# Differential heads weighed two at a time, with their scores in one run, out of one pool of six PSUM banks

## The chip, the cores and the metric

The kernel runs on one core of one Trainium2 chip. The metric is the device time of one execution in microseconds. The kernel before takes 2825.22 us, the median of three runs (2824.94 to 2826.13).

Engines are named as in the profile: PE is TensorE, PEld its weight loads, DVE is VectorE, ACT is ScalarE, POOL is GpSimd, SP is SyncE, which issues most DMAs here.

## The reference

A two-layer encoder for one sequence of 256 tokens with 2048 features, all in float32. Each layer runs two kinds of attention side by side on the same normed input, gates both, adds them to the stream, and then runs a SwiGLU feed-forward and a small gated embedding. What matters here is the first half of a layer:

```python
z = h @ w_in[i]          # [diff q | diff k | diff v | q-latent | kv-latent | rope key | gate_diff | gate_mla]
# A: differential attention, 8 heads, two softmax maps of 64 dimensions each
scores  = jnp.einsum('bqhcd,bkhcd->bhcqk', qb, kh) * 64 ** -0.5
probs   = jax.nn.softmax(scores, axis=-1)
weights = probs[:, :, 0] - lam * probs[:, :, 1]
od      = jnp.einsum('bhqk,bkhe->bqhe', weights, v)
od      = rmsnorm(od, g_subln[i], SUBLN_EPS) * (1.0 - lam_init)
# B: latent attention, 8 heads; q_nope, q_rope from the q-latent, k_nope, v from the kv-latent
scores  = (q_nope @ k_nope.T + q_rope @ k_rope.T) * 192 ** -0.5
merged  = sigmoid(ga) * (A @ w_branch_diff) + sigmoid(gb) * (B @ w_branch_mla)
x       = x + merged @ w_out[i]
```

## The kernel before

The stream is kept transposed: 16 tiles of 128 features by 256 tokens. Every large product has the weights as the stationary operand and the tokens as the moving one. To keep float32 accuracy with products of float32r, each number is split into a high and a low part. A tile of tokens holds both parts side by side (512 columns). For each block of 128 x 128 weights PE issues two matmuls: the weights' high part (`whi`) against all 512 columns (L226) and the weights' low part (`wlo`) against the 256 columns of the high part (L230). `product` does this over the 16 blocks of a column of weights, 32 matmuls into one PSUM bank; `joined` adds the two halves of that bank with an ACT copy and a DVE add.

Weights come in pieces of up to 1024 columns: SP issues the DMA, ACT writes `whi` (L201), DVE writes `wlo = w - whi` (the subtraction in `tt`, L78). There are four buffers for the raw piece and three for each part. PE can't start a piece before both parts are there, and ACT can't make the next `whi` before PE has let a buffer go.

The order on each engine is not the order of the program. A planner, run when the program is built (`schedule_with_timeline_sim=True`), goes through a simulated time with its own costs and at each step issues, for each engine, the earliest instruction of the program that is ready by then, if its buffer is free. Two helpers tie it: `keep_in_program_order` puts an instruction behind the one traced just before it on the same engine, and `issue_after` puts a block behind a given instruction.

In the attention stage of a layer these steps occur:

- `queries_keys(h)`: two products (queries and keys of a differential head), each followed by the partial rotary turn on DVE and the split into high and low part.
- `keys_up(n)`: two heads' keys of the latent attention, two short products of two blocks each.
- `queries_up(n)`: two heads' queries of the latent attention, two products of four blocks each.
- `gate`: a product and a scaling. Seven of them stand in this stage or right behind it, the others beside the latent heads.
- the shared rotary key: `narrow` (L414), then `rotated`.
- `settle(h0)`: the norm of four finished differential heads, with eight transposes (L716).

A differential head goes through `diff_weights` and `diff_out`. `diff_weights` computes two maps of scores, one from partitions 0 to 63 and one from 64 to 127 of the same tiles. Each map takes six matmuls with 64 rows (three products of high and low parts for each half of the queries), and the two maps alternate, so a head has a run of 12 (L428). Each map fills a bank of its own. Then DVE takes the row maxima (L434), ACT the exponentials with their sums (L437), DVE the reciprocals (L438), and the two maps are combined into `E[0]` (ACT L691, DVE in `stt`, L81). `diff_out` transposes the weights on PE (L446), copies them (ACT L451), multiplies with the values (PE L701) and takes the squares for the norm.

`pipelined` sets the order: the scores of head h + 1 are traced before the transposes of head h. The generator `beside` is asked for one step before the scores and one between the transposes and the outputs of each head, so that products stand in both places. The first scores come right after the queries and keys of head 1, before any step of `beside`.

PSUM has eight banks: four in the pool `ps_mm` for products and values, two in `ps_s` for scores, two in `ps_at` for transposes and outputs. The very end of the kernel takes two of the `ps_s` banks again for the transposes of the result.

Of the kernel before, what the change touches and what calls it, by code (L numbers as in the profile page):

```python
# [16 lines left out]
ALU = mybir.AluOpType  # L17
# [39 lines left out]
def encoder(ctx, tc, x, p, positions, cols, lams, wq, wk, wv, wcq, wckv, wkr, wga, wgb,  # L57
# [6 lines left out]
    wts = pool("wts")  # L64
    tmp = pool("tmp")
    stat = pool("stat")
    ps_mm = pool("ps_mm", 4, space=PSUM)
    ps_s = pool("ps_s", 2, space=PSUM)
    ps_at = pool("ps_at", 2, space=PSUM)

    def scratch(tag, bufs, n=T):
# [2 lines left out]
    def bank(ps=ps_at, tag="at", name="at", shape=(P, 2 * T)):  # L74
        return ps.tile(list(shape), F32, tag=tag, name=name)
# [178 lines left out]
    def joined(acc, o=None):  # L254
        t = scratch("join", 3)
        A.activation(t, acc[:, T:], AF.Copy)  # L256
        o = scratch("a", 4) if o is None else o
        tt(o, acc[:, :T], t, ALU.add)
        return o
# [117 lines left out]
    def rotated(a, c_, s_, o=None):  # L377
        if o is None:
            r = bank()[:, :T]
            PE.matmul(r, halves, a, start=True, stop=True)  # L380
        else:
            r = a
        t = scratch("sh", 2)
        V.stream_shuffle(t, r, SWAP16)
        tt(t, t, s_, ALU.mult)
        tt(a, r, c_, ALU.mult)
        tt(a, a, t, ALU.add)
        if o is None:
            hi, rest = krs
            A.activation(hi[:, :T], a, AF.Copy)  # L390
            for j in range(2):
                s, t = slice(64 * j, 64 * j + 64), slice(j * T, (j + 1) * T)
                tt(rest[s, t], a[s], hi[s, :T].bitcast(F32), ALU.subtract)
        else:
            A.activation(o.rearrange("p (h t) -> p h t", h=2), a.rearrange("p (h t) -> p h t", h=1).to_broadcast([P, 2, T]), AF.Copy)
            for j in range(2):
                s, t = slice(64 * j, 64 * j + 64), slice(j * T, (j + 1) * T)
                tt(o[64 - 64 * j : 128 - 64 * j, t], a[s], o[s, t].bitcast(F32), ALU.subtract)

    def narrow(src, us):  # L400


        acc = bank(ps_mm, "mm", "mm")
        w = wts.tile([P, PT * P], F32, tag="w32", name="w32", bufs=W_BUFS)
        nc.sync.dma_start(w, src)
        w = w.rearrange("p (c m) -> p c m", m=64)
        for a in range(0, NC, PT):
            both = wts.tile([P, PT * P + 64], F32R, tag="whi", name="whi", bufs=3)[:, : PT * P]
            hi, lo = (both.rearrange("p (c f m) -> p c f m", f=2, m=64)[:, :, f, :] for f in range(2))
            part = w[:, a : a + PT, :]  # L410
            A.activation(hi, part, AF.Copy)
            tt(lo, part, hi.bitcast(F32), ALU.subtract)
            for j in range(PT):
                PE.matmul(acc, both[:, j * P : (j + 1) * P], us[a + j], start=a + j == 0, stop=a + j == NC - 1)  # L414
        return acc
# [1 line left out]
    def three(q, k):  # L417
        return [(q[:, :T], k[:, T:]), (q[:, T:], k[:, :T]), (q[:, :T], k[:, :T])]

    def scores(*maps):  # L420


        Ss = [bank(ps_s, "S", "S", (P, 2, T)) for _ in maps]
        for b in range(2):
            for j in range(len(maps[0])):
                for S, pairs in reversed(list(zip(Ss, maps))):
                    q, k = pairs[j]
                    PE.matmul(S[:, b, :], q[:, b * P : (b + 1) * P], k, start=j == 0, stop=j == len(pairs) - 1)  # L428
        return Ss

    def exps(S, E, scale):
# [95 lines left out]
    for L in range(DEPTH):  # L527
# [45 lines left out]
        def queries_keys(h, *inside):  # L573
            for which, w in enumerate((wq, wk)):
                a = joined(product(w[L, h], ua, inside=(8, inside[which]) if inside else None))
                sh = scratch("sh", 2)
                V.stream_shuffle(sh, a, ROPE16)
                tt(sh, sh, sr, ALU.mult)
                tt(a, a, cr, ALU.mult)
                tt(a, a, sh, ALU.add)  # L580
                split(qk[h][which], a)
# [18 lines left out]
        def keys_up(n):  # L600
            for acc in pair(w_kn[L, n : n + 2], ckv):
                kn.append(operand(fb(len(kn), F32R)))
                split(kn[-1], joined(acc))
# [19 lines left out]
        queries_keys(0, lambda: lcols.append(norm([skv], KVR)), lambda: lcols.append(norm([sq], QR)))  # L623
        queries_keys(1, lambda: latent_norm(ckv, "g_kv_latent", rkv, lcols[0]), lambda: latent_norm(cq, "g_q_latent", rq, lcols[1]))

        def beside():

            for h in range(2, DH):
                if h < 6:
                    keys_up(2 * h - 4)  # L630
                elif h == 7:
                    rotated(joined(narrow(wkr[L], ua)), crm, srm)
                yield
                queries_keys(h)
                yield
            for n in (8, 0, 2, 10):
                if n == 0:
                    settle(0)
                gate(wga, gate_a, next(todo))
                queries_up(n)  # L640
                yield
            settle(4)
            for n in (4, 6):
                gate(wga, gate_a, next(todo))
                queries_up(n)
            gate(wga, gate_a, next(todo))

        def gate(w, store, n):
            tt(store(n), joined(product(w[L, n], ua)), R, ALU.mult)
# [27 lines left out]
            tc.add_manual_dep(si.ins, last_exp[0].ins.name, NO_SYNC, reason="one change of tables")  # L677


        fill = beside()  # L680
        od, ods = [], ub[:8]
        ssd = stat.tile([P, 2 * DH], F32, tag="ssd", name="ssd", bufs=1)

        def diff_weights(h):
            q, k = qk[h]
            E = [weights(), weights("E1")]
            halves = [slice(c * 64, (c + 1) * 64) for c in range(2)]
            r = [exps(S, e, 0.125) for S, e in zip(scores(*(three(q[d], k[d]) for d in halves)), E)]
            ts(r[1], r[1], neg_lam[:, L : L + 1], None, ALU.mult)
            for b in range(2):  # L690
                A.activation(E[0][:, b, :], E[0][:, b, :], AF.Copy, scale=r[0][:, b : b + 1])  # L691
                stt(E[0][:, b, :], E[1][:, b, :], r[1][:, b : b + 1], E[0][:, b, :], ALU.mult, ALU.add)
            return E[0]

        def diff_out(h, W):
            wt = turned(W)
# [30 lines left out]
                next(out, None)  # L727
                W = nxt

        pipelined(diff_weights, diff_out, DH, lambda: next(fill, None))  # L730
        for _ in fill:
            pass
        vm, = (v for v in values(w_v[L], ckv) if v is not None)


# [1 line left out]
        def mla_weights(h):  # L737
            E = weights()
            t = slice(h % 2 * T, (h % 2 + 1) * T)
            S, = scores(three(qn[h], kn[h]) + [(qr[h // 2][:, t], krs[1][:, t]), (qr[h // 2][:, t], krs[0][:, :T])])  # L740
            r = exps(S, E, MLA_SCALE)
            for b in range(2):
                ts(E[:, b, :], E[:, b, :], r[:, b : b + 1], None, ALU.mult)
            return E
# [176 lines left out]
    def store(b, q, o):  # L921
        tc.keep_in_program_order(nc.sync.dma_start(out[b, :, q * 2 * T : (q + 2) * 2 * T], o))

    def S_bank():
        return operand(bank(ps_s, "S", "S", (P, 2, T)))

    def mm_bank():
        return bank(ps_mm, "mm", "mm")

    def steps(which, n):  # L930
        for _ in range(n):
            tc.keep_in_program_order(next(which))
# [6 lines left out]
    column = factors(0)  # L939
    for which, n in ((column, 2), (third, 1), (second, 2), (third, 2), (column, 2)):  # L940
        steps(which, n)
    t0 = [transposed(0, q, get()) for q, get in enumerate((S_bank, S_bank, mm_bank, mm_bank))]
    t1 = [transposed(1, 0, mm_bank())]
    column = factors(1)
    t1.append(transposed(1, 1, mm_bank()))
# [6 lines left out]
    for j in range(2):  # L952
        tc.keep_in_program_order(scaled(parts_[j][:, right], t0[2 * j + 1], cols_[0], V))
        steps(column, 2)
        store(0, 2 * j, parts_[j])
    t1.append(transposed(1, 3, S_bank()))
    for j in range(2):
        tc.keep_in_program_order(scaled(parts_[2 + j][:, left], t1[2 * j], cols_[1], V))
        scaled(parts_[2 + j][:, right], t1[2 * j + 1], cols_[1], A)
# [89 lines left out]
```

## Time and profile before

| | |
|---|---|
| Time, median of three runs | 2825.22 us (2824.94 to 2826.13) |
| Profiled execution: its own time | 2825.27 us |
| Profiled execution: span, first to last instruction | 2823.5 us |
| Granted clock of TensorE | 0.999 |
| Busy: PE / PEld / DVE / ACT | 2815.7 / 2489.4 / 2080.0 / 1532.0 us |
| Matmuls with 64 rows (scores of the differential heads) | 192, in 16 runs of 12 |
| Differential stage, first layer | about 106 to 207 us from the span's start |
| The same, second layer | about 1510 to 1611 us |

Rows of the order of time give start, duration, engine, line and operation, the tiles written and read, shapes, and a count where neighbours are merged. The end of a matmul is modelled, and matmuls overlap, so the time that one holds PE is read from its start to the start of the next. Tile names are those of the program: `ua` and `ub` are the two sets of token tiles, `mm` and `S` PSUM banks, `at` a bank of `ps_at`. Rows of waits give who waited, for whom, the sum in us, the count and the longest. Rows that group instructions give the count, then the busy time and the mean in ns, then the idle time ahead of them.

### The profile page before, as it was taken

To read this page: it belongs to the slowest core of one execution; us is meant where nothing else is said; L and a number is where in the kernel's file an instruction comes from. 1 tells how busy PE (TensorE), PEld (TensorE's weight loads), DVE (VectorE), ACT (ScalarE), POOL (GpSimd) and SP (SyncE) were. 2 spreads that over 40 slices of the span, in tenths; PEclk is the share of its full clock that TensorE was granted. 3 is DMA by queue.
4 is the path that set the end of the run, shared out by engine and by line. 5 is a ranking of instruction groups with operands and counts; after the bars stand their busy time and mean duration, and the time that the engine had idled before them with its cause. 6 is when DMAs were issued, how large, how long until landed. Compare 5 with 4: busy or idle time off the path is not lost.

```text
span 2823.5 us, 43989 instructions
## 1 busy us (share of the span) xinstructions
PE 2815.7 (100%) x16691; PEld 2489.4 (88%) x16691; DVE 2080.0 (74%) x3566; ACT 1532.0 (54%) x2554; POOL 3.1 (0%) x17
## 2 busy tenths in 40 slices
PE   9999999999999999999999999999999999999999
PEld 8888988888888888888888889888888888888888
DVE  8898668776666666677869976687766666666777
ACT  7676546554444444455646765465544444444556
POOL 0000000000000000000000000000000000000000
PEclk9999999999999999999999999999999999999999
DMA  7545455555665566566554454555556655655654
GB/s 247 174 162 172 157 187 198 194 193 194 186 200 193 188 195 197 193 193 193 194 193 166 157 172 158 194 198 193 194 193 189 199 193 185 202 194 194 193 193 157
DMA packets 158180, 531.36 MB, mean 188 GB/s; under 512 B 17168, under 2 KB 25360, under 8 KB 157968
## 3 DMA queue, kind: packets, MB, share of 16 engines
q1 hardware_dynamic: 157536, 527.96, 56.8%
q8 instruction: 131, 2.15, 0.3%
q10 hardware_dynamic: 432, 0.59, 0.1%
q14 instruction: 81, 0.66, 0.1%
HBM read 526.39 MB, written 2.10 MB: 187 GB/s over the span
## 4 chain that ended last, share of the span: by engine, by line
PE 100%; DMA 0%; DVE 0%; ACT 0%; DVEq 0%; issue 0%
PE mm L226 61%; PE mm L230 31%; PE S L428 1%; PE mmv L501 1%; PE mmv L502 1%; PE mmv L503 1%; PE at L446 1%; PE at L701 1%; PE mm L848 0%; PE at L757 0%; PE mm L414 0%; PE at L716 0%; PE mmv L472 0%; DMA gcol<-in_cols 0%; PE at L339 0%; PE at L307 0%
## 5 line engine op out<-in xcount | busy, mean ns | idle before, releaser
L201 ACT ACTIVATE whi<-w 128x1024 fp32r<-128x1024 f32 (+2 forms) x1038 | 1064.3, 1026 | 1225.6 <-issue 592.8
L78 DVE TENSOR_TENSOR wlo<-w,whi 128x1024 fp32r<-128x1024 f32 (+2 forms) x1038 | 1225.7, 1181 | 645.7 <-ACT whi L201 635.1
L226 PE MATMUL mm<-ub,whi 128*128 128x512 f32 x3936 | 1340.5, 389 | 0.0
L226 PE MATMUL mm<-ua,whi 128*128 128x512 f32 x3712 | 1274.8, 390 | 0.0
L230 PE MATMUL mm<-ub,wlo 128*128 128x256 f32 x3936 | 1084.6, 276 | 0.0
L230 PE MATMUL mm<-ua,wlo 128*128 128x256 f32 x3712 | 1027.8, 277 | 0.0
L226 PEld LDWEIGHTS mm<-ub,whi 128*128 128x128 f32 x3936 | 737.7, 188 | 152.4
L226 PEld LDWEIGHTS mm<-ua,whi 128*128 128x128 f32 x3712 | 696.2, 188 | 141.2
L230 PEld LDWEIGHTS mm<-ub,wlo 128*128 128x128 f32 x3936 | 738.8, 188 | 1.3
L230 PEld LDWEIGHTS mm<-ua,wlo 128*128 128x128 f32 x3712 | 697.0, 188 | 1.9
L78 DVE TENSOR_TENSOR a<-mm,join 128x256 f32<-128x256 f32 (+1 forms) x423 | 174.9, 417 | 1.7 <-ACT join L877 1.4
L256 ACT ACTIVATE join<-mm 128x256 f32<-128x256 f32 x452 | 165.8, 368 | 6.5 <-PE mm L230 5.8
L78 DVE TENSOR_TENSOR xT<-xT,mm 128x256 f32<-128x256 f32 x256 | 106.9, 420 | 41.5 <-PE mm L230 37.6
L78 DVE TENSOR_TENSOR a<-a,row 128x256 f32<-128x256 f32 (+1 forms) x209 | 87.6, 422 | 5.9
L78 DVE TENSOR_TENSOR a<-a 128x256 f32<-128x256 f32 x120 | 50.9, 426 | 4.0
L78 DVE TENSOR_TENSOR ua<-a,ua 128x256 fp32r<-128x256 f32 x120 | 50.0, 418 | 1.0 <-ACT ua L264 1.0
L264 ACT ACTIVATE ua<-a 128x256 fp32r<-128x256 f32 x120 | 48.2, 403 | 2.6 <-DVE a L78 2.6
L437 ACT ACTIVATE E<-S,nm 128x256 f32<-128x256 f32 x96 | 44.2, 472 | 8.1 <-DVE nm L84 8.0
L501 PE MATMUL mmv<-whi,ua 128*128 128x512 f32 x124 | 47.2, 392 | 0.0
L502 PE MATMUL mmv<-whi,ua 128*128 128x512 f32 x124 | 47.0, 392 | 0.0
L503 PE MATMUL mmv<-wlo,ua 128*128 128x512 f32 x124 | 41.2, 391 | 0.0
L78 DVE TENSOR_TENSOR ssq<-ssq,sq 128x256 f32<-128x256 f32 x96 | 40.2, 419 | 0.3 <-ACT sq L294 0.3
(214 smaller groups left out, 1211.6 us busy)
## 6 DMA issues: line engine op xcount, KB each, us to landing
w<-in_w_gate SPq DMA_DIRECT2D x176, 512.0 KB, 4.5
w<-in_w_up SPq DMA_DIRECT2D x176, 512.0 KB, 4.6
w<-in_w_down SPq DMA_DIRECT2D x128, 512.0 KB, 4.2
w<-in_wga SPq DMA_DIRECT2D x64, 512.0 KB, 3.7
w<-in_wgb SPq DMA_DIRECT2D x64, 512.0 KB, 3.7
w<-in_w_out SPq DMA_DIRECT2D x64, 512.0 KB, 3.9
w<-in_w_pg SPq DMA_DIRECT2D x64, 512.0 KB, 4.7
w<-in_w_down SPq DMA_DIRECT2D x64, 384.0 KB, 3.6
```

The source lines that it names most:

```text
L78: return V.tensor_tensor(out=o, in0=a, in1=b, op=op)
L201: last_split[:] = A.activation(hi[:, s], w[:, s], AF.Copy), tt(lo[:, s], w[:, s], hi[:, s].bitcast(F32), ALU.subtract)
L226: lead = PE.matmul(acc, hi[:, s], u, start=start, stop=False)
L230: rest = PE.matmul(acc[:, T:], lo[:, s], u[:, :T], start=False, stop=stop)
L256: A.activation(t, acc[:, T:], AF.Copy)
L264: return A.activation(hi, src, AF.Copy), tt(lo, src, hi.bitcast(F32), ALU.subtract)
L428: PE.matmul(S[:, b, :], q[:, b * P : (b + 1) * P], k, start=j == 0, stop=j == len(pairs) - 1)
L437: last_exp[0] = A.activation(E[:, b, :], S[:, b, :], AF.Exp, bias=nm[:, b : b + 1], scale=scale, accum_out=sm[:, b : b + 1])
L446: PE.transpose(tp[:, kb, b * P : (b + 1) * P], W[:, b, kb * P : (kb + 1) * P], ident)
L501: PE.matmul(banks[k][b], xh, hi[:, s], start=c == 0, stop=False)
L502: PE.matmul(banks[k][b], xl, hi[:, s], start=False, stop=False)
L503: last_mm[:] = [PE.matmul(banks[k][b], xh, lo[:, s], start=False, stop=c == n - 1)]
```

## The change

The two pools `ps_mm` and `ps_s` become one of six banks, and scores take their banks from it. `diff_weights` takes two heads at once: `scores` allots four banks and issues the 12 matmuls of head h0 + 1 and then the 12 of head h0, each tied to the one before with `keep_in_program_order`. The softmax of both follows, then both heads' transposes and, later, both heads' outputs.

`beside` and the use of `pipelined` for these heads are replaced by a list written out. Queries and keys of head 2, the first `keys_up` and queries and keys of head 3 come before the first scores. Each pair has products between its scores and its transposes and again between its transposes and its outputs. The shared key stands beside the third pair, behind two gates, and `settle(0)` comes behind the scores of the last pair. The latent heads keep `pipelined`; their scores come from the pool of six, and are not tied. At the end of the kernel the transposes take banks of this pool.

```diff
-    ps_mm = pool("ps_mm", 4, space=PSUM)
-    ps_s = pool("ps_s", 2, space=PSUM)
+    ps_mm = pool("ps_mm", 6, space=PSUM)
...
-    def scores(*maps):
...
-        Ss = [bank(ps_s, "S", "S", (P, 2, T)) for _ in maps]
-        for b in range(2):
-            for j in range(len(maps[0])):
-                for S, pairs in reversed(list(zip(Ss, maps))):
-                    q, k = pairs[j]
-                    PE.matmul(S[:, b, :], q[:, b * P : (b + 1) * P], k, start=j == 0, stop=j == len(pairs) - 1)
+    def mm_bank():
+        return bank(ps_mm, "mm", "mm")
+
+    def S_bank():
+        return mm_bank().rearrange("p (b t) -> p b t", b=2)
...
+    def scores(*heads):
...
+        Ss = [[S_bank() for _ in maps] for maps in heads]
+        for banks, maps in zip(Ss, heads):
+            for b in range(2):
+                for j in range(len(maps[0])):
+                    for S, pairs in reversed(list(zip(banks, maps))):
+                        q, k = pairs[j]
+                        m = PE.matmul(S[:, b, :], q[:, b * P : (b + 1) * P], k, start=j == 0, stop=j == len(pairs) - 1)
+                        if len(heads) > 1:
+                            tc.keep_in_program_order(m)
         return Ss
...
-        def beside():
-
-            for h in range(2, DH):
-                if h < 6:
-                    keys_up(2 * h - 4)
-                elif h == 7:
-                    rotated(joined(narrow(wkr[L], ua)), crm, srm)
-                yield
-                queries_keys(h)
-                yield
-            for n in (8, 0, 2, 10):
-                if n == 0:
-                    settle(0)
-                gate(wga, gate_a, next(todo))
+        def shared_key():
+            rotated(joined(narrow(wkr[L], ua)), crm, srm)
+
+        def gate_and_queries(n=None):
+            gate(wga, gate_a, next(todo))
+            if n is not None:
                 queries_up(n)
-                yield
-            settle(4)
-            for n in (4, 6):
-                gate(wga, gate_a, next(todo))
-                queries_up(n)
-            gate(wga, gate_a, next(todo))
...
-        def diff_weights(h):
-            q, k = qk[h]
-            E = [weights(), weights("E1")]
+        def diff_weights(h0):
             halves = [slice(c * 64, (c + 1) * 64) for c in range(2)]
-            r = [exps(S, e, 0.125) for S, e in zip(scores(*(three(q[d], k[d]) for d in halves)), E)]
...
+            pairs = [[three(qk[h][0][d], qk[h][1][d]) for d in halves] for h in (h0 + 1, h0)]
+            Ws = []
+            for Ss in scores(*pairs):
+                E = [weights(), weights("E1")]
+                r = [exps(S, e, 0.125) for S, e in zip(Ss, E)]
...
+                Ws.append(E[0])
+            return Ws[::-1]
...
-        pipelined(diff_weights, diff_out, DH, lambda: next(fill, None))
-        for _ in fill:
-            pass
+        def work(*steps_):
+            for act, *arg in steps_:
+                act(*arg)
+
+        def weighed_pair(h, beside, ahead):
+            Ws = diff_weights(h)
+            work(*beside)
+            outs = [diff_out(h + j, Ws[j]) for j in range(2)]
+            for part in outs:
+                next(part)
+            work(*ahead)
+            for part in outs:
+                next(part, None)
+
+        Q, K, G = queries_keys, keys_up, gate_and_queries
+        work((Q, 2), (K, 0), (Q, 3))
+        weighed_pair(0, ((Q, 4), (K, 2)), ((Q, 5),))
+        weighed_pair(2, ((Q, 6), (K, 4)), ((Q, 7),))
+        weighed_pair(4, ((G, 8), (G,)), ((shared_key,), (K, 6)))
+        weighed_pair(6, ((settle, 0), (G, 0), (G, 2)), ((G, 10),))
+        settle(4)
+        work((G, 4), (G, 6))
...
-            S, = scores(three(qn[h], kn[h]) + [(qr[h // 2][:, t], krs[1][:, t]), (qr[h // 2][:, t], krs[0][:, :T])])
+            (S,), = scores([three(qn[h], kn[h]) + [(qr[h // 2][:, t], krs[1][:, t]), (qr[h // 2][:, t], krs[0][:, :T])]])
...
-    t0 = [transposed(0, q, get()) for q, get in enumerate((S_bank, S_bank, mm_bank, mm_bank))]
+    t0 = [transposed(0, q, get()) for q, get in enumerate((mm_bank, mm_bank, mm_bank, mm_bank))]
...
-    t1.append(transposed(1, 3, S_bank()))
+    t1.append(transposed(1, 3, mm_bank()))
```

More of the change, by code (lines that the diff above doesn't have):

```diff
@@ L418, in three @@
         return [(q[:, :T], k[:, T:]), (q[:, T:], k[:, :T]), (q[:, :T], k[:, :T])]
-    def scores(*maps):
-        Ss = [bank(ps_s, "S", "S", (P, 2, T)) for _ in maps]
-        for b in range(2):
-            for j in range(len(maps[0])):
-                for S, pairs in reversed(list(zip(Ss, maps))):
-                    q, k = pairs[j]
-                    PE.matmul(S[:, b, :], q[:, b * P : (b + 1) * P], k, start=j == 0, stop=j == len(pairs) - 1)
+    def mm_bank():
+        return bank(ps_mm, "mm", "mm")
+    def S_bank():
+        return mm_bank().rearrange("p (b t) -> p b t", b=2)
+    def three(q, k):
+        return [(q[:, :T], k[:, T:]), (q[:, T:], k[:, :T]), (q[:, :T], k[:, :T])]
+    def scores(*heads):
[8 more added lines that the diff above has]
+                            tc.keep_in_program_order(m)
         return Ss
@@ L677, in sigmoid @@
             tc.add_manual_dep(si.ins, last_exp[0].ins.name, NO_SYNC, reason="one change of tables")
-        fill = beside()
         od, ods = [], ub[:8]
         ssd = stat.tile([P, 2 * DH], F32, tag="ssd", name="ssd", bufs=1)
-        def diff_weights(h):
-            q, k = qk[h]
-            E = [weights(), weights("E1")]
+        def diff_weights(h0):
             halves = [slice(c * 64, (c + 1) * 64) for c in range(2)]
-            r = [exps(S, e, 0.125) for S, e in zip(scores(*(three(q[d], k[d]) for d in halves)), E)]
[L689 to L693, printed above, removed]
+            pairs = [[three(qk[h][0][d], qk[h][1][d]) for d in halves] for h in (h0 + 1, h0)]
[3 more added lines that the diff above has]
+                r = [exps(S, e, 0.125) for S, e in zip(Ss, E)]
+                ts(r[1], r[1], neg_lam[:, L : L + 1], None, ALU.mult)
+                for b in range(2):
+                    A.activation(E[0][:, b, :], E[0][:, b, :], AF.Copy, scale=r[0][:, b : b + 1])
+                    stt(E[0][:, b, :], E[1][:, b, :], r[1][:, b : b + 1], E[0][:, b, :], ALU.mult, ALU.add)
+                Ws.append(E[0])
+            return Ws[::-1]
         def diff_out(h, W):
@@ L922, in store @@
         tc.keep_in_program_order(nc.sync.dma_start(out[b, :, q * 2 * T : (q + 2) * 2 * T], o))
[L924 to L928, printed above, removed]
     def steps(which, n):
```

## Prediction

> **What bounds the kernel now.** I read the page first: the engines, the granted clock and the chain that ended last.
>
> ```profile
> span 2823.5 us, 43989 instructions
> PE 2815.7 (100%) x16691; PEld 2489.4 (88%) x16691; DVE 2080.0 (74%) x3566; ACT 1532.0 (54%) x2554; POOL 3.1 (0%) x17
> PEclk9999999999999999999999999999999999999999
> PE 100%; DMA 0%; DVE 0%; ACT 0%; DVEq 0%; issue 0%
> ```
>
> PE is busy all through at full clock, and the whole chain runs over it. A busy share alone doesn't say that PE never waits, so the second view was the waits of PE:
>
> ```profile
> PE at L517 <- DVE ones L123: 1.1, 1, 1.1
> PE mmv L472 <- ACT whi L201: 0.3, 1, 0.3
> ```
>
> That is the whole answer: 1.4 us in 2823.5, all in the first microseconds. So the time is the sum of what PE issues, start to start. A change can gain only where PE itself loses time between matmuls, and can lose wherever it makes PE wait. The third view was the order of time on PE around the scores of the differential heads (L428). The columns are start, duration, engine, line, operation, tiles, shapes, count.
>
> ```profile
> 105.68 0.39 PE L226 MATMUL mm<-ua,whi 128*128 128x512 f32 x1
> 105.91 0.28 PE L230 MATMUL mm<-ua,wlo 128*128 128x256 f32 x1
> 106.02 0.39 PE L226 MATMUL mm<-ub,whi 128*128 128x512 f32 x1
> 106.25 0.28 PE L230 MATMUL mm<-ub,wlo 128*128 128x256 f32 x1
> 106.45 0.96 PE L428 MATMUL S<-fa,ub 64*128 64x256 f32 x12
> 107.35 0.50 PE L226 MATMUL mm<-ub,whi 128*128 128x512 f32 x1
> 107.69 0.28 PE L230 MATMUL mm<-ub,wlo 128*128 128x256 f32 x1
> ```
>
> Undisturbed, a hi matmul takes 0.23 us start to start (105.68 to 105.91) and a lo matmul 0.11 (105.91 to 106.02). The run of 12 stretches its neighbours too: the lo before it holds 0.20 (106.25 to 106.45), the hi behind it 0.34 (107.35 to 107.69). From 106.25 to 107.69 are 1.44 us; less 0.11 and 0.23 the run costs 1.10. Inside the run the matmuls start two by two, one for each half of 64 rows:
>
> ```profile
> 106.45 0.39 PE L428 MATMUL S<-fa,ub 64*128 64x256 f32 x2
> 106.67 0.52 PE L428 MATMUL S<-fa,ub 64*128 64x256 f32 x6
> 106.80 0.51 PE L428 MATMUL S<-fa,ub 64*128 64x256 f32 x6
> 107.14 0.28 PE L428 MATMUL S<-fa,ub 64*128 64x256 f32 x2
> ```
>
> The pairs start at 106.45, 106.67, 106.80 and so on to 107.14: the first holds 0.22, the last 0.21 until 107.35, those from 106.80 to 107.14 0.34/3 = 0.113 each. Six pairs at 0.113 are 0.68 us, so **entering and leaving a run costs 1.10 - 0.68 = 0.42 us**. Where transposes follow instead of a product:
>
> ```profile
> 138.31 0.28 PE L230 MATMUL mm<-ua,wlo 128*128 128x256 f32 x1
> 138.51 0.96 PE L428 MATMUL S<-fa,ub 64*128 64x256 f32 x12
> 139.41 0.66 PE L446 MATMUL at<-ident,E 128*128 128x128 f32 x4
> 139.82 0.47 PE L226 MATMUL mm<-ua,whi 128*128 128x512 f32 x1
> 284.21 0.60 PE L446 MATMUL at<-ident,E 128*128 128x128 f32 x4
> 284.56 0.47 PE L226 MATMUL mm<-ua,whi 128*128 128x512 f32 x1
> ```
>
> Lo and run take 1.10 (138.31 to 139.41), the run so 0.99; the four transposes take 0.41 against 0.35 for a group with no run of 64 rows ahead (284.21 to 284.56), 0.06 more. The run costs 1.05, its entry and exit 0.37.
>
> Heads 6 and 7 are followed by products, as head 0 is:
>
> ```profile
> 193.04 0.97 PE L428 MATMUL S<-fa,ub 64*128 64x256 f32 x12
> 193.95 0.38 PE L230 MATMUL mm<-ua,wlo 128*128 128x256 f32 x1
> 206.65 0.96 PE L428 MATMUL S<-fa,ub 64*128 64x256 f32 x12
> 207.54 0.39 PE L230 MATMUL mm<-ua,wlo 128*128 128x256 f32 x1
> ```
>
> **The change part by part.** *Pairs of heads, 24 scores in a run.* A layer has eight runs of 12 now: three with a product behind (heads 0, 6, 7), five with transposes: 3 x 0.42 + 5 x 0.37 = 3.11 us. Afterwards it has four runs of 24: the scores themselves cost the same (12 pairs at 0.113), the entries and exits are four. The code puts products behind each run, so 4 x 0.42 = 1.68. Two layers: 2 x (3.11 - 1.68) = **2.9 us gained**. If transposes follow, it is 2 x (3.11 - 1.48) = 3.3. No run of two heads is in the trace, so the joint between the heads is unknown: between nothing (the pairs at 0.113 go on over the change of bank inside a head) and a whole entry, 0.42, which would take the gain to nothing. I take nothing, because both heads use the same two halves of 64 rows.
>
> *What a stop leaves behind.* Products go at two speeds:
>
> ```profile
> 109.90 0.40 PE L226 MATMUL mm<-ua,whi 128*128 128x512 f32 x1
> 110.25 0.40 PE L226 MATMUL mm<-ua,whi 128*128 128x512 f32 x1
> 131.62 0.39 PE L226 MATMUL mm<-ua,whi 128*128 128x512 f32 x1
> 131.96 0.39 PE L226 MATMUL mm<-ua,whi 128*128 128x512 f32 x1
> ```
>
> A hi and lo pair takes 0.35 us in the first two rows and 0.34 in the last two. The slow step begins at an interruption and lasts until the next. Between a run and the next transposes now lie up to 36 pairs of products (queries 16, keys 16, keys_up 4): 36 x 0.01 = 0.36 us for each of eight runs, 2.9 in all. So this is worth anything from +2.9 (every run leaves the slow step, none did before) to about -2.9 (the reverse). As both kernels interrupt as often with transposes and outputs, I take nothing.
>
> *First two steps later, shared key and gates moved, settling behind the last run.* Every product, weight DMA and transpose is still issued once; SP's queue only carries the weights in another order. They change no PE time as long as the halves of the weights are ready. That cover is DVE's work, and it is thin here:
>
> ```profile
> 106.00:210.00 104.00, 104.00 (x677) 90.80 (x675) 98.76 (x251) 77.47 (x196) 0.00 (x0) 1.00 0.49 163
> 106.00:124.00 18.00, 18.00 (x111) 15.49 (x109) 18.00 (x44) 15.34 (x35) 0.00 (x0) 1.00 0.48 150
> 223.00:260.00 37.00, 37.00 (x225) 32.85 (x224) 30.96 (x72) 23.04 (x44) 0.00 (x0) 1.00 0.54 183
> ```
>
> The columns are the stretch, its length, and busy time of PE, weight loads, DVE, ACT, POOL; then clock, DMA share and GB/s. DVE is busy 98.76 of 104 us, and without a pause from 106 to 124, where the first weighing meets the latent norms. Starting the weighing two steps later (queries and keys of heads 2 and 3, each head two products of 5.4 us) takes it from there and pushes the end towards the gates, where DVE has 6 us in 37 free. I price these moves at nothing; if the cover goes, the price is that of the slower rival.
>
> *Six banks in one pool.* It is 4 + 2 as before, but a pair of heads holds four and leaves two to products. Cover: a product of 16 pairs lasts 16 x 0.34 = 5.4 us, and its bank is emptied by one copy and one add of about 0.4 us each (next rows), so two banks rotate without a wait. If a third were wanted, PE would wait until an exponential has let a bank go. Behind the last run the six are the same six, so the tail stays.
>
> ```profile
> L256 ACT ACTIVATE join<-mm 128x256 f32<-128x256 f32 x25 | 9.0, 374 | 0.3 <-PE mm L414 0.2
> L434 DVE TENSOR_REDUCE nm<-S 128x2 f32<-128x512 f32 x16 | 10.3, 683 | 0.0
> L81 DVE SCALAR_TENSOR_TENSOR E<-E,rsum,E 128x256 f32<-128x256 f32 x14 | 6.2, 479 | 0.1
> ```
>
> **The sum.** The profiled execution took 2825.27 us (span 2823.5 and 1.8 around it), 0.05 over the median of the runs, 2825.22. 2825.27 - 2.9 = **2822.4 us**, 0.10% less. No change can be told from a difference under 0.2%, here 5.65 us, by a measurement of this kernel.
>
> **The rivals.** *Slower: two heads' softmax delays the weights.* DVE splits each piece of weights into its lo part and does the maxima and the weighing. One head costs it 2 x 0.683 + 2 x 0.479 = 2.3 us by the rows above. A lo piece is ready this much ahead:
>
> ```profile
> 132.94 1.23 DVE L78 TENSOR_TENSOR wlo<-w,whi 128x1024 fp32r<-128x1024 f32 x1 [0.32 <-ACT whi L201]
> 135.93 0.28 PE L230 MATMUL mm<-ua,wlo 128*128 128x256 f32 x1
> ```
>
> Ready at 134.17, used at 135.93: 1.76 us. If a second head's 2.3 us stand ahead of it, PE waits 0.5 us a run, and behind it wait all products. With a maximum, an exponential and a bank each late in turn, I take three such pieces a pair: 8 x 3 x 0.5 = 12 us, less 2.9: 2834. It eats the gain from 2.9/8 = 0.36 us a run on. For it speaks DVE's 95%; against it, that PE consumes no piece during the 1.6 us of a double run, that the two heads' work is spread over two steps of products, and the removal of the 106 to 124 pile-up. The Trainium skill, TensorEngine Tiling (Array Packing), Performance Considerations, warns of just this: tiling speeds up TensorE, but not the emptying of PSUM, which may become the bound. The trace of before shows no such wait of PE.
>
> *No gain: the runs are cut.* The pins tie a score only to the PE instruction traced before it; a product with an earlier place in the program may still be put between the scores when its weights come. Eight cuts at 0.37 give back 2.9: 2825.3. For it: outputs already stand in the middle of a product; against it, all runs of 12 are whole with no pin at all. The slow step of 0.35 at every run gives the same time.
>
> *Hidden anyway.* DVE with 95% could set the pace of this stage; then PE's gain turns into waiting, 2825.3 again. Against it: the 1.76 us above and PE without a wait in either layer. By the Trainium skill, Perfetto Trace Analysis, Identifying the Most-Contended Engine, TensorE's headroom is judged by the share of weight loads, not of matmuls; that is 88% here, so there would be headroom and this rival would hold. The waits of PE disagree, and a measured wait decides over a share.
>
> *More.* The slow step goes as well: 2825.3 - 2.9 - 2.9 = 2819.5.
>
> **How the numbers follow.** Forecast 0.62, cut runs or slow step 0.18, hidden 0.06, slower 0.09, more 0.05. The forecast's own range is 2821.3 to 2824.0. To hold eight in ten, the range reaches over the no-gain cases and most of the way to the larger gain: 2820.3 to 2826.2; the slower rival is left out. Faster by over 0.2% means under 2819.6: 0.04, most of *more*. Slower by over 0.2% means over 2830.9: 0.07, most of the slower rival. Within: 0.89.
>
> **What would show it.** Right: eight runs of 24 with 64 rows, each some 1.58 us long (0.90 + 6 x 0.113) with the same stretched neighbours, and PE's list of waits as short as now. Wrong: scores x12 or x18 in the order of time (cut), a PE wait for DVE's wlo or for an exponential between 106 and 260 us (slower), a first pair of 0.2 us in the middle of a run (the joint), or more products at 0.35. A gain over 4 us or any loss would say that something outside the runs moved.

## The result, and the profile after

The changed kernel takes **2833.79 us** (median of seven runs, 2832.29 to 2834.1), the kernel before 2825.22 in as many: a ratio of 1.0028, 95% interval 1.0018 to 1.0038. It is 8.6 us slower. The forecast was 2822.4, so 11.4 us have to be found. The ranges given below leave out two executions that stand far outside all others, one of `key_first` (8438.87 us) and one of the kernel before (3520.82 us).

The page of the changed kernel, the lines that answer to those of before:

```profile
span 2831.9 us, 43909 instructions
PE 2817.0 (99%) x16691; PEld 2493.8 (88%) x16691; DVE 2078.6 (73%) x3566; ACT 1534.3 (54%) x2554; POOL 3.1 (0%) x17
PEclk9999999999999999999999999999999999999999
PE 97%; DVE 2%; ACT 1%; issue 0%; DVEq 0%
```

PE has as many matmuls as before and is busy for nearly the same time, 2817.0 us against 2815.7, but the span has grown by 8.4, and 3% of the chain that ended last is no longer PE's. The waits of PE (for whom, sum, count, longest) say why:

```profile
PE at L379 <- DVE a L77: 3.8, 2, 1.9
PE mm L229 <- DVE wlo L77: 2.6, 4, 0.9
PE at L700 <- ACT fa L703: 1.1, 2, 0.6
PE at L528 <- DVE ones L122: 1.1, 1, 1.1
```

Only the last was there before. The others, 7.5 us, are new, and each comes in both layers. The runs themselves came out as forecast. The order of time on PE in the changed kernel, around the first run:

```profile
129.49 0.28 PE L229 MATMUL mm<-ua,wlo 128*128 128x256 f32 x1
129.70 1.65 PE L437 MATMUL mm<-fa,ub 64*128 64x256 f32 x24
131.27 0.50 PE L225 MATMUL mm<-ua,whi 128*128 128x512 f32 x1
131.61 0.28 PE L229 MATMUL mm<-ua,wlo 128*128 128x256 f32 x1
```

From 129.49 to 131.61 are 2.12 us. Less 0.11 for the lo and 0.23 for the hi matmul the run costs 1.78; twelve pairs at 0.113 are 1.36, so entry and exit cost 0.42, and the joint between the heads costs nothing. All eight runs are whole. Read the same way, start to start with the neighbours at their undisturbed price, the sixteen runs of before hold PE for 17.1 us and the eight runs of now for 14.3: 2.8 us less, where 2.9 were forecast.

The longest of the new waits is that of the shared key's rotation. First PE, then DVE:

```profile
208.80 0.28 PE L229 MATMUL mm<-ub,wlo 128*128 128x256 f32 x1
211.00 1.07 PE L379 MATMUL at<-a,rc 128*128 128x256 f32 x2 [1.92 <-DVE a L77]
211.86 1.91 PE L700 MATMUL at<-vals,wt 128*128 128x128 f32 x8
214.25 1.31 PE L700 MATMUL at<-vals,wt 128*128 128x128 f32 x8 [0.47 <-ACT fa L703]
```

```profile
208.75 1.74 DVE L77 TENSOR_TENSOR ub<-a,ub 64x256 fp32r<-64x256 f32 x4
210.52 0.42 DVE L77 TENSOR_TENSOR a<-mm,join 128x256 f32<-128x256 f32 x1
```

The key's matmuls are all issued by 208.0. DVE then does four splits for the queries of the latent attention, 1.74 us, and only at 210.52 the add that the rotation needs. On PE only `keys_up(6)`, which is short, stood between the key and the third pair's outputs, and it has already been issued. So PE stands from 208.91 to 211.00, 2.1 us. The outputs of the two heads come next and want a bank that ACT has not emptied, 0.5 us more.

The waits for `wlo` lie behind the first run and behind the third, that of heads 4 and 5. First PE, then ACT and DVE before the first wait, and DVE before the second:

```profile
144.78 0.49 PE L457 MATMUL at<-ident,E 128*128 128x128 f32 x3
146.13 0.39 PE L229 MATMUL mm<-ua,wlo 128*128 128x256 f32 x1 [0.86 <-DVE wlo L77]
...
186.89 1.69 PE L437 MATMUL mm<-fa,ub 64*128 64x256 f32 x24
...
200.36 0.39 PE L229 MATMUL mm<-ua,wlo 128*128 128x256 f32 x1 [0.44 <-DVE wlo L77]
```

```profile
142.98 2.04 ACT L200 ACTIVATE whi<-w 128x1024 fp32r<-128x1024 f32 x2
...
144.13 0.48 DVE L80 SCALAR_TENSOR_TENSOR E<-E,rsum,E 128x256 f32<-128x256 f32 x1
144.52 0.42 DVE L77 TENSOR_TENSOR a<-a,fc 128x256 f32<-128x256 f32 x1
144.86 1.22 DVE L77 TENSOR_TENSOR wlo<-w,whi 128x1024 fp32r<-128x1024 f32 x1
...
196.19 1.07 DVE L83 TENSOR_SCALAR fa<-fa,ry 128x128 f32<-128x128 f32 x5
...
197.26 0.66 DVE L83 TENSOR_SCALAR fa<-fa,ry 128x128 f32<-128x128 f32 x3
```

The first is of the kind that the slower rival described: work for two heads stands ahead of the split. It is ACT's as much as DVE's: ACT writes this piece's `whi` only from 142.98 to about 144.0, behind eight exponentials (136.68 to 140.4), and DVE then has a last weighing and a step of the rotary turn ahead of `wlo`. The second is not: the eight scalings of `settle(0)`, 1.07 and 0.66 us, stand there, amid the softmax of the third pair. In the program `settle(0)` comes behind the scores of the fourth pair, which run at 215.49; the planner issued it a whole pair earlier, since its inputs were ready.

### The profile page after: what moved, and what is told of

The parts are those of the page before. It is cut to its first block, busy times and chain, and to the rows that moved or that the text cites. A ratio compares the mean times of both kernels' runs of the same rounds, so it can differ in the third digit from the quotient of the medians.

```text
span 2831.9 us, 43909 instructions
## 1 busy us (share of the span) xinstructions
PE 2817.0 (99%) x16691; PEld 2493.8 (88%) x16691; DVE 2078.6 (73%) x3566; ACT 1534.3 (54%) x2554; POOL 3.1 (0%) x17
## 4 chain that ended last, share of the span: by engine, by line
PE 97%; DVE 2%; ACT 1%; issue 0%; DVEq 0%
PE mm L225 60%; PE mm L229 30%; PE mmv L513 1%; PE mmv L514 1%; PE mmv L512 1%; PE mm L437 1%; DVE wlo L77 0%; PE at L700 0%; PE mm L866 0%; PE at L775 0%; PE at L457 0%; ACT E L448 0%; DVE a L77 0%; ACT whi L200 0%; DVE E L80 0%
## 5 line engine op out<-in xcount | busy, mean ns | idle before, releaser
L448 ACT ACTIVATE E<-mm,nm 128x256 f32<-128x256 f32 x96 | 44.2, 475 | 21.5 <-DVE nm L83 21.4
```

The lines of the kernel that those rows point to most:

```text
L448: last_exp[0] = A.activation(E[:, b, :], S[:, b, :], AF.Exp, bias=nm[:, b : b + 1], scale=scale, accum_out=sm[:, b : b + 1])
```

## The experiments

Unless said otherwise an edit is made to the changed kernel. Times are medians of 9 to 11 runs (4 for `pool_only` and `two_pools`), with their lowest and highest; ratios are to runs of the kernel before on the same chip.

**Which of the moves costs what.** `key_first` puts the shared key ahead of the two gates instead of behind them:

```diff
-        weighed_pair(4, ((G, 8), (G,)), ((shared_key,), (K, 6)))
+        weighed_pair(4, ((shared_key,), (G, 8), (G,)), ((K, 6),))
```

> The changed kernel with one edit: in the third pair the shared key stands ahead of the two gates instead of behind them. Theory (shared key): behind the gates its last product ends with no product left on PE, and its DVE add stands behind the rope splits of the queries; PE waits 2.1 us for it, runs the next matmuls more slowly in one layer, and then waits for the bank of the first output. Those rows make 4.7 us in the first layer and 3.0 in the second, so this run should take 2833.8 - 7.7 = 2826.1 us, with no wait of PE at the rotation's matmul (L379). Rival (double softmax): the burst of two heads' softmax is what costs, wherever the wait falls; then the run stays above 2831 us, and the waits for wlo or for the exponentials grow instead.

Measured: 2829.05 (2828.33 to 2829.34), ratio 1.0012 (1.0003 to 1.0022). That is **4.7 us** back, where 7.7 were expected. Its one kind of wait of PE behind the start, and DVE's order behind the third run:

```profile
PE mm L229 <- DVE wlo L77: 3.6, 4, 0.9
```

```profile
196.83 1.65 DVE L83 TENSOR_SCALAR fa<-fa,ry 128x128 f32<-128x128 f32 x8
198.40 2.35 DVE L77 TENSOR_TENSOR wlo<-w,whi 128x1024 fp32r<-128x1024 f32 x2
```

The rotation's wait is gone, and the outputs' wait with it. The waits for `wlo` have grown by 1.0 us, because the scalings of `settle(0)` now stand in one block ahead of the split. That is 1.0 of the 3.0 us that are missing; the other 2.0 are not accounted for. `settle_tied` keeps this edit and ties `settle(0)` behind the weighing of the last pair, whose last instruction `last_weighed` holds:

```diff
+        def settle_behind(h0):
+            with tc.issue_after(last_weighed[0].ins):
+                settle(h0)
...
-        weighed_pair(6, ((settle, 0), (G, 0), (G, 2)), ((G, 10),))
+        weighed_pair(6, ((settle_behind, 0), (G, 0), (G, 2)), ((G, 10),))
```

> The run with the shared key first (2829.05 us), and DVE's part of the first settling (a rsqrt and eight scalings, some 3 us) tied behind the last weighing of the last pair, as its place in the program says. Theory: these scalings stand ahead of wlo at 197 us, and PE waits 1.1 us a layer there; tied, that wait goes: 2829.05 - 2.2 = 2826.9 us, the first pair's 1.03 us a layer stays. Rival: the wait moves to the next piece and the time stays within 0.7 us.

Measured: 2826.25 (2825.9 to 2827.25), ratio 1.0003 (0.9994 to 1.0013), **2.8 us** less than `key_first`, where 2.2 were expected. The scalings now run behind the fourth run, and one wait a layer is left:

```profile
PE mm L229 <- DVE wlo L77: 1.7, 2, 0.9
...
235.09 1.66 DVE L83 TENSOR_SCALAR fa<-fa,ry 128x128 f32<-128x128 f32 x8
```

**The wait behind the first run.** Two edits were to break up the burst of two softmaxes. `second_later` is `key_first` with the second head's softmax traced inside the first product behind the run, and `both_ties` is `settle_tied` with it:

```diff
-                Ws.append(E[0])
-            return Ws[::-1]
+                yield E[0]
...
-            Ws = diff_weights(h)
-            work(*beside)
+            weighing = diff_weights(h)
+            Ws = [next(weighing)]
+            work(*beside(lambda: Ws.insert(0, next(weighing))))
```

> The run with the shared key first (2829.05 us), and the softmax of the second head of each pair traced in the middle of the first product behind the run instead of right behind the first head's. Theory (burst): eight exponentials in one go keep ACT from whi, and the weighing of both heads keeps DVE from wlo; broken in two, the wait of 1.03 us a layer for wlo behind the first pair's transposes goes: 2829.05 - 2.1 = 2827.0 us. Rival (the wait comes from too little lead at that place, whatever the order of the softmax): 2829 us or more, with the wait still there.

> Both edits. If each takes its own wait away, 2829.05 - 2.1 - 2.2 = 2824.8 us, below the kernel before (2825.35). If the two waits have one cause, DVE and ACT with too little spare time in this stage, at most one of them goes: 2827 us or more.

Measured: `second_later` 2829.10 (2828.86 to 2829.99), ratio 1.0013 (1.0004 to 1.0023), the same as `key_first`; `both_ties` 2825.98 (2825.54 to 2826.59), ratio 1.0002 (0.9993 to 1.0012), within 0.3 us of `settle_tied`. A miss: the waits for `wlo` are the same to the tenth. In `both_ties` ACT does the eight exponentials in one go as before, from 136.20 to 139.8, so the tie to that product held nothing back: the planner issues what is ready, and a later place in the program is not by itself a later time.

So the other way was tried: give PE a product there whose weights are ready. `gate_early` and `gate_late` take the plain gate from the third pair in `both_ties` to the first, ahead of the products or behind them (the edit shown is that of `gate_early`, against `both_ties`):

```diff
-        weighed_pair(0, lambda second: ((Q, 4, second, nothing), (K, 2)), ((Q, 5),))
+        weighed_pair(0, lambda second: ((G, None, second), (Q, 4), (K, 2)), ((Q, 5),))
...
-        weighed_pair(4, lambda second: ((shared_key,), (G, 8, second), (G,)), ((K, 6),))
+        weighed_pair(4, lambda second: ((shared_key,), (G, 8, second)), ((K, 6),))
```

> The run with both ties (2825.98 us), and the gate without queries moved from the third pair to the front of the first pair's products. What is left there is one wait a layer of 1.03 us for wlo behind the first pair's transposes, where ACT is busy without a pause for 10 us before. Theory (too little spare time of ACT and DVE beside two heads' softmax): a gate's product needs less of both than queries and keys, so 5.4 us of such a product ahead let them catch up; the wait goes and the long runs' gain shows: 2825.98 - 2.1 = 2823.9 us, 1.4 under the kernel before. Rival (the wait sits at the change from transposes to products, whatever lies ahead): 2826 us, with the wait still there.

> The same, with the gate between keys_up and the transposes. By the theory the gate's 5.4 us come after the burst and give the pieces behind it the same time: 2823.9 us as well. By the rival 2826 us.

Measured: 2829.15 (2828.96 to 2830.16) and 2831.36 (2831.09 to 2832.4), ratios 1.0013 (1.0004 to 1.0023) and 1.0021 (1.0012 to 1.0031): both slower than `both_ties`, where 2823.9 had been expected. The waits of PE in `gate_early`:

```profile
PE mm L225 <- ACT E L448: 2.8, 2, 1.4
PE mm L225 <- DVE a L77: 2.5, 2, 1.3
```

The wait for `wlo` is gone in `gate_early` and stays in `gate_late` (1.7 us), so the place ahead of the first products is the one that helps. But the gate is now missing in the third pair, and the products behind the last run wait for a bank, for an exponential (L448) or an add, 5.3 us in all. `gate_from_end` therefore takes a gate from behind the stage:

```diff
-        weighed_pair(0, ((Q, 4), (K, 2)), ((Q, 5),))
+        weighed_pair(0, lambda second: ((G, None, second), (Q, 4), (K, 2)), ((Q, 5),))
...
-        work((G, 4), (G, 6))
+        work((G, 4), (queries_up, 6))
```

It keeps the third pair's gates, with `key_first` and `settle_behind`. `end_no_hook` is the same without `second`.

> The run with both ties (2825.98 us), with one gate's product at the front of the first pair as in the run before, but taken from the very end of the stage, so that the third pair keeps its own gate and the banks have the same time to come free ahead of the last scores. Theory (two separate prices: the burst, paid for by a product with little work for ACT and DVE, and the four banks, paid for by products between the last keys and the scores): neither the wait for wlo (1.03 us a layer) nor the wait for a bank (2.8 us a layer) is there, and the long runs' gain shows at last: 2825.98 - 2.1 = 2823.9 us, 1.5 under the kernel before. Rival (each gate moved only moves the wait): 2826 us or more, with a new wait of PE.

> gate_from_end with the second head's softmax traced right behind the first's, as in the changed kernel, instead of inside the first product behind the run. Theory (second_later changed nothing, since the planner issues by readiness; what took the last wait away is the gate's product between the run and the first piece of weights): 2823.0, between 2822.4 and 2823.8, and no PE wait behind the start. Rival (the second head's place in the program is needed too): a PE wait of 0.5 to 1.0 us a layer on wlo again, 2824.0 to 2825.0.

Measured: `gate_from_end` **2823.00** (2822.4 to 2823.85), ratio 0.9991 (0.9982 to 1.0); `end_no_hook` 2823.23 (2823.04 to 2823.56), ratio 0.9992 (0.9983 to 1.0001). Each interval touches 1, but the runs do not overlap with those of before, 2825.08 at the least in the one comparison and 2824.8 in the other: 2.5 and 2.4 us faster. The only wait of PE over 0.2 us is the start's, and between 106 and 214 us PE is never idle. `gate_from_end` and, below it, the changed kernel (stretch, length, busy PE, PEld, DVE, ACT, POOL, clock, DMA share, GB/s):

```profile
PE at L528 <- DVE ones L122: 1.1, 1, 1.1
...
106.00:214.00 108.00, 108.00 (x687) 95.35 (x686) 96.70 (x230) 74.76 (x173) 0.00 (x0) 1.00 0.50 164
```

```profile
106.00:214.00 108.00, 104.55 (x654) 91.59 (x652) 99.08 (x249) 75.58 (x177) 0.00 (x0) 0.99 0.49 161
```

DVE is 90% busy in the one and 92% in the other. The share hardly moves; what moved is the order of DVE's steps and which products PE has beside them. Since `end_no_hook` does as well, the second head's place in the program is not needed.

**Are the long runs worth what they were priced at?** `cut_runs` puts one transpose between the two heads' scores in the changed kernel, `end_cut` does so in `gate_from_end`. Nothing reads it, and nothing is left out.

```diff
+            if len(heads) > 1 and banks is Ss[1]:
+                tc.keep_in_program_order(PE.transpose(bank()[:, :P], ident, ident))
```

> The changed kernel with one transpose of the identity (128 rows, nobody reads it) between the two heads' scores, so that there are sixteen runs of 12 again. Theory (each entry and exit costs 0.37 to 0.42 us of PE time): eight more of them and eight transposes of 0.11 us, 8 x (0.37 + 0.11) = 3.8 us more, 2837.6 us. Rival (the entries are hidden under the waits of this stage, so that the long runs gain nothing): less than 1 us more, 2834 to 2835.

> gate_from_end with one transpose that nobody reads between the scores of the two heads, so 16 runs of 12 again. Theory (the long runs are what gate_from_end gains on the kernel before; nothing else in it waits): in cut_runs a pair of heads took 2.30 us (1.149 + 1.152) instead of 1.82, 0.48 more each, so 8 x 0.48 = 3.8 us more: 2823.0 + 3.8 = 2826.8, and PE's waits stay at the 1.1 us of the start. Rival (the gain comes from the other order of products and gates, and the long runs are worth little): less than 1 us more, at most 2824.0. As in cut_runs the planner may deal the rest out otherwise: a PE wait behind 106 us would say so, and then the time is read as PE's busy sum less the waits.

Measured: `cut_runs` 2831.91 (2831.2 to 2832.77), ratio 1.0023 (1.0014 to 1.0033): **1.9 us faster** than the changed kernel, which neither theory had. Its trace points to why: the planner dealt the rest out anew, PE's waits behind the start fell from 7.5 to about 4 us (the rotation's alone from 3.8 to 1.1), and the stretch at half clock that the last section describes isn't there. The two together outweigh the cuts. A control in a kernel that is full of waits tells nothing of the runs. `end_cut` is the one that does: 2828.53 (2828.16 to 2829.73), ratio 1.0011 (1.0002 to 1.002), 5.5 us slower than `gate_from_end`, where 3.8 were expected. Its one wait of PE behind the start, and a cut run:

```profile
PE at L434 <- ACT fa L703: 0.9, 2, 0.5
...
129.89 0.28 PE L229 MATMUL mm<-ua,wlo 128*128 128x256 f32 x1
130.10 0.97 PE L439 MATMUL mm<-fa,ub 64*128 64x256 f32 x12
130.99 0.33 PE L434 MATMUL at<-ident 128*128 128x128 f32 x1
131.26 0.96 PE L439 MATMUL mm<-fa,ub 64*128 64x256 f32 x12
132.15 0.50 PE L225 MATMUL mm<-ua,whi 128*128 128x512 f32 x1
132.49 0.28 PE L229 MATMUL mm<-ua,wlo 128*128 128x256 f32 x1
```

From lo to lo this takes 2.60 us, the whole run 2.12: 0.48 more, of which 0.11 is the transpose itself and 0.37 the second entry. Eight of them are 3.8 us, the transposes' own wait for a bank (L434) is 0.9, and 0.8 is not accounted for. Without the transposes' 8 x 0.11 that leaves 8 x 0.37 = 3.0 us for the entries, beside the 2.9 that were predicted. The sum over all runs, as above, is 14.5 us in `gate_from_end`, 2.6 less than in the kernel before.

**What one pool of six does by itself.** `pool_only` is the kernel before with this edit alone (and the transposes at the end take their banks from the same pool); `pipelined` and `beside` stay:

```diff
-    ps_mm = pool("ps_mm", 4, space=PSUM)
-    ps_s = pool("ps_s", 2, space=PSUM)
+    ps_mm = pool("ps_mm", 6, space=PSUM)
...
-        Ss = [bank(ps_s, "S", "S", (P, 2, T)) for _ in maps]
+        Ss = [bank(ps_mm, "mm", "mm").rearrange("p (b t) -> p b t", b=2) for _ in maps]
```

> The kernel before with its two pools made one of six banks, nothing else. Theory: the pool costs nothing, 2825.2 us within 1 us, runs of 12 as before and no new wait of PE. Rival: one pool lets the planner order PE, DVE and ACT otherwise and makes PE wait; then 2 us or more above the kernel before.

Measured: **2907.98** (2907.57 to 2909.47), ratio 1.0293 (1.0276 to 1.0311), 82.6 us slower, where no change was expected. Its waits, and its order of time on PE behind the first scores:

```profile
PE mm L428 <- DVE fa L78: 21.5, 8, 4.4
PE at L446 <- DVE E L81: 18.1, 2, 9.1
...
108.82 0.28 PE L230 MATMUL mm<-ub,wlo 128*128 128x256 f32 x1
118.15 1.21 PE L446 MATMUL at<-ident,E 128*128 128x128 f32 x4 [9.04 <-DVE E L81]
119.28 1.65 PE L428 MATMUL mm<-fa,ub 64*128 64x256 f32 x12
```

After the first scores and `keys_up(0)` PE issues no product for 9.3 us, until the transposes and the next scores have gone. In the kernel before, products filled this place. In this trace no product that the program has behind a run of scores passes it. The reading is that banks of one pool are handed out in the order of the program, so a product traced behind scores that wait for their operands has no bank, though banks are free. `two_pools` was to test this from the other side, the changed kernel with two banks for products and four for scores:

```diff
-    ps_mm = pool("ps_mm", 6, space=PSUM)
+    ps_mm, ps_s = pool("ps_mm", 2, space=PSUM), pool("ps_s", 4, space=PSUM)
...
-        return mm_bank().rearrange("p (b t) -> p b t", b=2)
+        return bank(ps_s, "S", "S").rearrange("p (b t) -> p b t", b=2)
```

The values' products and the transposes at the end take some of their banks from `ps_s` too.

> The changed kernel with its six banks parted again: four for the scores (and the second half of the values), two for products. Theory (one line for the banks): with one pool a product traced behind a score gets no bank before that score has its own, so PE has nothing to issue while it waits; parted, products pass and the wait at the rotation's matmul (L379, 3.8 us in both layers, with the slow matmuls behind it) is filled: 2827 to 2830 us. Rival (two banks are too few for products, or the order doesn't hang on the banks): 2833 us or more.

Measured: 2928.77 (2917.48 to 2932.32), ratio 1.0359 (1.0338 to 1.038). Its waits of PE:

```profile
PE mm L225 <- DVE a L77: 29.1, 15, 3.1
PE mm L225 <- DVE xT L77: 13.4, 19, 1.9
```

Products do pass scores here, and the rotation's wait is down to about 0.5 us a kernel. But two banks are too few for products all through the kernel, in the feed-forward too (`xT`), so its time says nothing of the order. **That banks are handed out in program order is supported by where the products stand in both traces, and not isolated.**

## Why the prediction was wrong

*The bound* held: the time is what PE issues plus what it waits, and the experiments moved with PE's list of waits. Only the stretch at half clock, some 1.5 us, had no term.

*The runs* were right: 0.42 us for entry and exit with products on both sides, nothing for the joint, eight whole runs of 24 lasting 1.57 to 1.61 us (1.58 forecast), and for all of them 2.8 us less in the changed kernel and 2.6 in `gate_from_end` (2.9 forecast). With the waits removed the kernel takes 2823.0, beside the forecast of 2822.4, and that is 2.5 us under the kernel before.

*The slow step of products*, taken as nothing between -2.9 and 2.9, was nothing as far as the traces show. What each product holds above 0.2265 us (hi) and 0.113 (lo), summed over the products that have products on both sides and no wait, is 8.5 us before, 8.8 after and 8.5 in `gate_from_end`.

*The step that failed* is "I price these moves at nothing", with the cover of DVE's work on the weights: moving the shared key and `settle(0)` cost 4.7 and 2.8 us, and the wait behind two heads' weighing another 3.0 (the wait itself, start to start, is 1.03 a layer). Taken apart in a row of three edits:

| kernel | edit added | us | step |
|---|---|---|---|
| changed kernel | | 2833.79 | |
| `key_first` | shared key ahead of the gates | 2829.05 | -4.7 |
| `settle_tied` | `settle(0)` behind the last weighing | 2826.25 | -2.8 |
| `end_no_hook` | a gate ahead of the first products | 2823.23 | -3.0 |

These are 10.5 of the 11.4 us. (The rows were timed on different chips; the kernel before took 2825.2 to 2825.7 us there.) The first two edits undo what the moves did. The third undoes no move: it gives PE other work where two heads' softmax holds the weights up, which is the slower rival's wait, once a layer. The working asked only whether halves of weights are ready. It did not follow the shared key: its product, ACT's copy, DVE's add, the rotation on PE. That is a chain, and PE stands at the rotation until it is through (208.91 to 211.00 above) unless other products are put ahead of the rotation. The order of time on PE before:

```profile
182.02 1.40 PE L414 MATMUL mm<-ua,whi 128*128 128x512 f32 x5
189.01 0.59 PE L380 MATMUL at<-a,rc 128*128 128x256 f32 x2
```

The key's last five matmuls are issued by about 183.2, and products of other heads fill the 5.8 us to the rotation; after, `keys_up(6)` stands there, two products of two blocks each. Nor did it ask when the planner would issue `settle(0)`, which is ready a pair before its place in the program, nor who is queued on DVE behind its eight scalings of 0.21 us.

*"Six banks in one pool", at nothing,* held in the new order and not in the old. `gate_from_end` has the pool of six, and PE doesn't wait in it; the same pool in the kernel before costs 82.6 us. The working counted the banks in use at once and the time to empty one. It did not ask in which order a shared pool gives them out, and so didn't see that the pool depends on the order written out beside it, whose scores have their operands ready when their turn comes. The two edits cannot be priced apart.

*The rivals.* "Slower" gave 2834 and the kernel takes 2833.8, but for the most part by another way. Its mechanism, the weighing of two heads ahead of a split of weights, is there once a layer, behind the first run, at 1.0 us (145.10 to 146.13, 144.78 with three transposes at 0.11 behind it), not three times a pair. The wait behind the third run is `settle(0)`'s, and the largest is the key's. The number was hit by chance; the chance given to it, 0.09, was too small, since DVE's 95% in this stage had been read and no other step of it was followed. "Cut runs" did not happen. "Hidden anyway" is refuted by `gate_from_end`: with DVE 90% busy, PE goes without a wait. The rule cited with it, from the Trainium skill, Perfetto Trace Analysis, Identifying the Most-Contended Engine, would judge PE's headroom by weight loads: they are 88% busy in the kernel before, after, and in `gate_from_end`, so here this share does not tell the kernel with PE's waits from those without. The other rule cited, on the emptying of PSUM, has its case in the outputs' wait for a bank, 1.1 of the 7.5 us of waits.

## What to carry to other kernels

Where one engine is the bound and never waits, a move "costs nothing" only after each chain that crosses to another engine and back has been followed at its new place: what PE still has to issue while it runs, and what stands ahead of it in the other engine's queue. A shared pool of buffers can change the order, not only the number. And a part's gain is measured with a control only in a kernel that doesn't wait elsewhere: the same cut made one kernel 1.9 us faster and the other 5.5 us slower.

## What the runs showed of the hardware

In the changed kernel the clock granted to PE halved after a stop of 1.92 us. It changes in steps of 3.41 us: ahead of the kernel's end three of the fourteen traces have stretches at half rate (this one, `pool_only`, `two_pools`), and all of them last 3.41, 6.83 or 10.24 us. These are such steps around the rotation's wait, three in the first layer and two in the second (columns as above: the clock stands behind POOL, ahead of the DMA share):

```profile
207.78:211.19 3.41, 1.49 (x9) 1.08 (x8) 3.29 (x7) 3.23 (x6) 0.00 (x0) 1.00 0.61 215
211.19:214.60 3.41, 2.94 (x11) 2.47 (x11) 3.41 (x8) 1.18 (x4) 0.00 (x0) 0.50 0.50 172
214.60:218.01 3.41, 3.41 (x39) 3.12 (x39) 2.89 (x7) 2.71 (x12) 0.00 (x0) 1.00 0.54 178
...
1617.48:1620.89 3.41, 1.59 (x10) 1.35 (x10) 3.34 (x7) 1.97 (x5) 0.00 (x0) 1.00 0.47 156
1620.89:1624.30 3.41, 2.98 (x35) 2.73 (x36) 3.41 (x10) 2.94 (x13) 0.00 (x0) 1.00 0.73 227
```

In the first layer the whole stop lies in one step, which has 1.92 us without a matmul, and the next step has half the clock; eight outputs then take 1.91 us instead of 1.05. In the second layer the stop begins ahead of the step, 1.82 us of it fall inside, and the clock stays full. The other traces agree: of the full-rate steps of all fourteen, the 18 with 1.87 us of idle PE or more are followed by half rate, none with 1.66 or less is, and of two in between one is (1.816) and this one (1.823) isn't. So about half a step of idle is enough; matmul ends are modelled, which leaves the border that uncertain.

The times of the changed kernel fall into two groups that fit this: four of 2833.8 to 2834.1 at a mean clock of 0.999, three of 2832.3 to 2832.7 at 1.000, 1.5 us apart. That the groups differ by this one step is inferred, since only one execution has a trace, and executions of the kernel before show both means too. By the Trainium skill, TensorE: Matmul & The Clock Gate, The HAM clock gate (the "warmup" mystery), the array falls to half rate after at least one idle window of about 3.4 us, and the windows run free of the kernel's start. The half rate (0.50), the length of a window (3.41) and its free run agree with the traces, and would explain why the same stop costs clock in one layer and not in the other. That the whole window must be idle does not: here 1.92 us of it were enough. For a kernel that keeps PE busy, a stop of some 2 us can thus cost 1.5 us more than itself, depending on how it falls on these steps.
